# A two-layer encoder trunk on one core: the first four output tiles of four dense stages made row tile by row tile

## The chip, the core and the metric

The kernel runs on one core of a Trainium2 chip. The metric is the device time of one execution in microseconds, the median of the runs, lower is better. Weights, inputs and constants lie in device memory and are read in every execution.

## What is computed

Two layers over S = 256 tokens of width D = 2048. Layer 0 mixes tokens with a sparse attention, layer 1 with RWKV-7; behind each stands a squared-ReLU MLP of width 4·D. Every sub-layer is normalised, modulated by a conditioning vector and added to the residual:

```python
hmix = rms_norm(x) * (1 + sc1) + sh1
x = x + g1 * (dsa_mixer(hmix, ...) if i % 2 == 0 else rwkv7_mixer(hmix, ...))
hff = rms_norm(x) * (1 + sc2) + sh2
x = x + g2 * (jnp.square(jax.nn.relu(hff @ mlp_w1[i])) @ mlp_w2[i])
```

Of the RWKV mixer two projections matter here, `r = xr @ w_r` and `k = xk @ w_k`, with `xr = h + delta * mu[0]` and `xk = h + delta * mu[2]`, where `delta` is the token before minus the token. All products are taken with float32 accuracy.

## The kernel before, in words

**Tiles.** x and every activation lie transposed: 16 row tiles of 128 features by 256 tokens. A value is split into a high part that TensorE multiplies exactly and a low rest, so one term of a product is three matmuls: high weight by high activation (L184), high by low (L185), low by high (L186). Split tiles are called A, and o for the last four of a stage; plain ones B. `dense` (L188) makes one output tile of 128 features: it goes through all 16 row tiles of the input, 48 matmuls into one PSUM bank. So the first output tile can't be finished before the last input tile is there.

**Weights.** `Weights` (L84 to L97) brings a weight in pieces of 128 rows by 512 columns, 256 KB each: a DMA issued by SyncE, a cast to the high part on ScalarE (L92), a subtraction for the low part on VectorE or GpSimd (L94). In the MLPs, pieces 2 and 3 of every four are GpSimd's. High and low tiles live in a ring of 8 slots named w, in the MLPs with 2 more named x (tiles whi, wlo, xhi, xlo). For a stage of `dense` the host lays a weight out so that the 4 pieces of a load hold the 16 row tiles of one output tile.

**The MLP** (`mlp`, L341). The input tiles h are x times a scale, made on ScalarE (high, L355) and VectorE (low, L356) straight from the residual; the RMS factor is put in behind the matmul. `tally` (L287) sums the squares of x into ssq on GpSimd. `up` (L366) makes an output tile with `dense` and then, in the very first tile only, calls `rms` (L371): four small matmuls sum ssq over the partitions (L306), VectorE scales the sum (L266), GpSimd takes the power -1/2 (L268), and four matmuls spread it over the partitions (L283) into a bank that is copied to rb. Each output tile is then multiplied by rb (L375), rectified, squared and split. Banks go round as d, c, m (2 + 2 + 2 banks). `ada_due` puts a part of the modulation of a later stage in between: a load of 1 MB and a row product on VectorE (L224).

**The RWKV projections** (`rwkv_project`, L717). `rms` gives rb in PSUM; `normed` (L728 to L731) multiplies x by rb on VectorE (L730) and modulates; `delta` (L735) is GpSimd's; `mix` (L738) is a VectorE operation (L741) and a split (L197 on ScalarE, L198 on VectorE or GpSimd). After the 16 mixed tiles `xm` of r, a loop over 16 output tiles makes r (banks d and m), stores it, and adds the row tile's part of four low-rank products (L770 to L772, banks a, b, i, j). Then 16 mixed tiles for the keys, and a loop in which output tile f of the keys is made (bank d) and `elements` (L851) of tile f - 1 works on it: it copies the bank to SBUF (L890) and has a chain of VectorE, ScalarE and GpSimd operations behind it; its own matmuls are L863 to L867 and a product of the gate. Value tiles follow.

**The order.** The program text gives dependences and banks; a list scheduler sets each engine's order from it at build time. It already lets up to four output tiles run side by side where their inputs come slowly. Each engine then works its list in order.

Of the kernel before, what the change touches and what calls it, by code (L numbers as in the profile page):

```python
# [16 lines left out]
P = 128  # L17
D = 2048
S = 256
NS = S + 2  # L20
NF = D // P
# [18 lines left out]
AHEAD_UP = 2  # L40
# [61 lines left out]
class Trunk:  # L102
# [85 lines left out]
    def dense(s, w, movs, cols):  # L188
# [3 lines left out]
        return p  # L192

    def split(s, full, hi_from=None, eng=None, t=None):
        if t is None:
# [145 lines left out]
    def mlp(s, layer):  # L341
# [23 lines left out]

        def up(b, f):  # L366
            w = s.wload(s.io["mlp_w1"][layer, b * 16 + f])
            s.ada_due()
            p = s.dense(w, h, cols)
            if b == f == 0:  # L370
                nc.scalar.copy(rb, s.rms(D, [s.ssq, s.lsq]))  # L371
            u, r, q = s.B(), s.B(), s.B()
# [46 lines left out]


        for b in range(4):
            for f in range(AHEAD_UP if b else 0, 16):
                up(b, f)
            for f in range(AHEAD_UP if b < 3 else 0):
                up(b + 1, f)
            for g in range(4):
                down(b, g)
# [289 lines left out]
    def rwkv_project(s, keep):  # L717
# [6 lines left out]
        for t in hp:  # L724
            nc.vector.memset(t[:, 0:1], 0.0)
        rb = s.rms(D, [s.ssq, s.lsq])

# [28 lines left out]
        hid = [s.bank(k) for k in "ccij"]  # L756
        s.xv = []
        for f in range(NF):
            w = s.wload(io["b_w_r"][f])
            p = s.dense(w, xm, cols)  # L760
            t = s.B()
# [26 lines left out]
        s.pc = keep.tile([P, NF, 4], F32, name="pc")  # L788
        xm = [mix(i, 2, t=s.O() if i >= NF - NO else None) for i in range(NF)]
        for f in range(NF + 1):  # L790
            if f < NF:
                w = s.wload(io["b_w_k"][f])
                pk = s.dense(w, xm, cols)
            if f:
# [56 lines left out]
    def elements(s, f, pk, omka, wa0):  # L851
# [36 lines left out]

        k, kk, sq = s.B(), s.B(), s.B()
        nc.scalar.copy(k, pk)  # L890
        nc.vector.tensor_scalar(kk, k, s.v("k_k", f), None, op0=OP.mult)
# [309 lines left out]
def layout(inputs):  # L1201
# [4 lines left out]
    vec = lambda a: a.reshape(-1, P).T  # L1206

    def tiles(w, rows, cols):

# [3 lines left out]
    a = {}  # L1213
# [15 lines left out]
    a["c"] = ct(g["c"].reshape(-1))  # L1229
    a["mlp_w1"] = np.stack([tiles(w, 16, P) for w in g["mlp_w1"]])  # L1230

# [18 lines left out]
    for n in ("a_w_o", "b_w_o"):  # L1250
        w = g[n][0]
        a[n] = np.concatenate([tiles(w[b * 512:(b + 1) * 512], 4, 512) for b in range(4)])
    for n in ("b_w_r", "b_w_k", "b_w_v"):
        a[n] = tiles(g[n][0], 16, P)
    l1 = np.concatenate([g["b_w_w1"][0], g["b_w_a1"][0], g["b_w_g1"][0]], 1)
# [24 lines left out]
```

## Time and profile before

| | us |
|---|---|
| median of 3 runs | 2749.15 |
| lowest and highest | 2748.52, 2752.12 |
| the profiled execution | 2751.64 |
| its span (first to last instruction) | 2749.5 |
| TensorE busy | 2587.6 (94%) |
| VectorE busy | 1946.8 (71%) |
| GpSimd busy | 1344.8 (49%) |
| ScalarE busy | 1312.8 (48%) |

All times that follow come from the one profiled execution and count from the start of its span. Its own time is 2.49 us above the median. PE is TensorE's matmuls, DVE VectorE, ACT ScalarE, POOL GpSimd, SP SyncE. The granted clock is the share of full speed that TensorE's clock ran at: 1.00 is 2.4 GHz, 0.50 is 1.2 GHz. A matmul record lasts longer than the distance to the next, since matmuls are pipelined; what counts is the distance, about 0.12 us at full clock and 0.215 us at half, for 256 or 258 columns. A time in brackets behind a row is how long the engine had stood idle, with the instruction that ended it. The first MLP's matmuls begin at 459.36, those of r at 1245.95, those of the keys at about 1387; the second MLP's stage begins at about 1997.

### The profile page before, as it was taken

The page shows a single profiled execution, that of the slowest core. Times are in us where ns is not written, and L with a number is a line of the kernel's source. Part 1 is how long each engine was busy: PE and PEld are TensorE (multiplying, and loading weights), DVE is VectorE, ACT ScalarE, POOL GpSimd, SP SyncE. Part 2 cuts the span into 40 slices and gives each one's busy share as a digit, 9 for nine tenths or more (in the row PEclk, how much of TensorE's full clock was granted, in tenths as well). Part 3 has the DMA queues.
Part 4 walks back from the last instruction along what each step waited for, and adds up shares of the span by engine and source line. Part 5 has one row for each costly group of instructions (what it writes and reads, how often), then busy time and mean ns, then how long its engine had stood idle before and what let it go on. Part 6 is the DMA issues. An engine that isn't in the chain of part 4 may idle for free. (4 is left out here: it accounts for less than half of the span.)

```text
span 2749.5 us, 58296 instructions
## 1 busy us (share of the span) xinstructions
PE 2587.6 (94%) x21876; PEld 2282.0 (83%) x21876; DVE 1946.8 (71%) x3135; ACT 1312.8 (48%) x2836; POOL 1344.8 (49%) x1121
## 2 busy tenths in 40 slices
PE   6898999999999999998989899999899999999997
PEld 3566778988979979877978888888799898898996
DVE  2256568999999999968887666766688377473553
ACT  3334435445445444446655434444455555454553
POOL 1343227557567575665655412223565445444453
PEclk9999999999999999998999899999999999999998
DMA  9987745889899899864656623332466667555553
GB/s 366 411 338 260 259 152 178 297 302 371 282 312 363 282 343 328 290 205 128 194 171 228 206 83 95 103 118 92 148 233 222 224 220 238 192 182 192 187 185 103
DMA packets 263595, 624.33 MB, mean 227 GB/s; under 512 B 29328, under 2 KB 43024, under 8 KB 238352
## 3 DMA queue, kind: packets, MB, share of 16 engines
q1 hardware_dynamic: 256400, 608.03, 63.8%
q10 hardware_dynamic: 6912, 12.59, 1.3%
q8 instruction: 171, 2.80, 0.4%
q14 instruction: 112, 0.92, 0.1%
HBM read 603.72 MB, written 16.78 MB: 226 GB/s over the span
## 5 line engine op out<-in xcount | busy, mean ns | idle before, releaser
L94 POOL TENSOR_TENSOR wlo<-raw,whi 128x512 fp32r<-128x512 f32 x364 | 587.2, 1622 | 586.7 <-ACT whi L92 445.6
L92 ACT CAST whi<-raw 128x512 fp32r<-128x512 f32 x856 | 514.8, 618 | 410.4 <-PE ps_d L185 117.1
L94 DVE TENSOR_TENSOR wlo<-raw,whi 128x512 fp32r<-128x512 f32 x492 | 443.0, 908 | 206.4 <-ACT whi L92 200.2
L94 POOL TENSOR_TENSOR wlo<-more,whi 128x512 fp32r<-128x512 f32 x181 | 265.7, 1470 | 341.6 <-ACT whi L92 218.2
L224 DVE CUSTOM_DVE_ANT_0 araw<-araw,cb 128x2048 f32<-128x2048 f32 x124 | 335.7, 2720 | 5.6 <-DMA araw<-ada_w_in 5.5
L92 ACT CAST whi<-more 128x512 fp32r<-128x512 f32 x366 | 223.6, 618 | 201.8 <-PE ps_m L397 43.3
L94 DVE TENSOR_TENSOR wlo<-more,whi 128x512 fp32r<-128x512 f32 (+1 forms) x185 | 168.4, 912 | 116.6 <-ACT whi L92 112.8
L184 PE MATMUL ps_d<-A,whi 128*128 128x256 f32 x656 | 197.9, 303 | 7.8 <-ACT B L890 4.0
L185 PE MATMUL ps_d<-A,whi 128*128 128x256 f32 x656 | 191.6, 293 | 4.0 <-DVE A L198 3.7
L186 PE MATMUL ps_d<-A,wlo 128*128 128x256 f32 x656 | 190.5, 291 | 0.0
L376 ACT ACTIVATE B<-B,sm 128x256 f32<-128x256 f32 x128 | 65.1, 508 | 239.9 <-DVE B L375 239.6
L185 PE MATMUL ps_d<-h,whi 128*128 128x258 f32 x560 | 160.1, 286 | 2.1 <-DVE h L356 2.1
L184 PE MATMUL ps_d<-h,whi 128*128 128x258 f32 x560 | 159.3, 285 | 0.0
L186 PE MATMUL ps_d<-h,wlo 128*128 128x258 f32 x560 | 158.4, 283 | 0.3 <-DVE wlo L94 0.2
L186 PE MATMUL ps_m<-h,wlo 128*128 128x258 f32 x532 | 150.9, 284 | 3.7 <-DVE wlo L94 3.7
L184 PE MATMUL ps_m<-h,whi 128*128 128x258 f32 x532 | 152.0, 286 | 0.0
L185 PE MATMUL ps_m<-h,whi 128*128 128x258 f32 x532 | 151.6, 285 | 0.0
L184 PEld LDWEIGHTS ps_d<-A,whi 128*128 128x128 f32 x656 | 129.9, 199 | 23.3 <-issue 5.0
L377 DVE TENSOR_TENSOR B<-B 128x256 f32<-128x256 f32 x128 | 109.8, 857 | 55.2 <-ACT B L376 55.2
L185 PEld LDWEIGHTS ps_d<-A,whi 128*128 128x128 f32 x656 | 129.9, 198 | 7.5 <-DVE A L198 6.1
L186 PEld LDWEIGHTS ps_d<-A,wlo 128*128 128x128 f32 x656 | 129.7, 198 | 0.7 <-issue 0.5
L395 PE MATMUL ps_d<-whi,A 128*128 128x512 f32 x300 | 118.4, 395 | 3.9 <-DVE B L375 3.5
(541 smaller groups left out, 8204.2 us busy)
## 6 DMA issues: line engine op xcount, KB each, us to landing
araw<-ada_w_in SPq DMA_DIRECT2D x192, 1024.0 KB, 6.9
raw<-mlp_w_in SPq DMA_DIRECT2D x614, 256.0 KB, 4.2
more<-mlp_w_in SPq DMA_DIRECT2D x410, 256.0 KB, 4.2
raw<-b_w_r_in SPq DMA_DIRECT2D x64, 256.0 KB, 3.3
raw<-b_w_k_in SPq DMA_DIRECT2D x64, 256.0 KB, 3.4
raw<-b_w_v_in SPq DMA_DIRECT2D x64, 256.0 KB, 3.5
raw<-b_w_o_in SPq DMA_DIRECT2D x64, 256.0 KB, 3.4
hd<-A ACTq DMA_DIRECT2D x48, 256.0 KB, 4.1
```

Source lines behind the costliest of these rows:

```text
L92: t.nc.scalar.copy(hi[:, :n], r)
L94: e.tensor_tensor(lo[:, :n], r, hi[:, :n].bitcast(F32), op=OP.subtract)
L184: mm(out, wh, m[:, :w], start=i == 0, stop=False)
L185: mm(out, wh, m[:, w:], start=False, stop=False)
L186: mm(out, wl, m[:, :w], start=False, stop=i == n - 1)
L224: nc.vector.tensor_tensor_reduce(out=w, in0=w, in1=s.cb, scale=1.0, scalar=0.0, op0=OP.mult, op1=OP.add, accum_out=acc[:, k:k + 1])
L376: nc.scalar.activation(r, u, AF.Relu, bias=c)
L377: nc.vector.tensor_tensor(q, r, r, op=OP.mult)
L395: nc.tensor.matmul(p, hi, wh, start=n == 0, stop=False)
```

## The change

A new helper makes four output tiles at once: row tile by row tile of the input, in each the three matmuls of every one of the four output tiles, in four banks. A row tile of the input is then used 12 times in a row. It is called at four places: for tiles 0 to 3 of each MLP's first block (banks d, d, a, b), of r and of the keys (banks d, d, m, m). The host lays the weights of those four tiles out anew: a piece holds one row tile of 128 rows and the 512 columns of all four output tiles. Their bytes and the number of matmuls are the same as before.

Three things move with it. In the MLPs `rms` and the copy of rb stand behind the four tiles, and the four tiles' own processing behind that; `ada_due` stands ahead of the weight load. In the r stage rb is copied to SBUF, since its bank is wanted, so L730 reads two SBUF tensors where it read one of SBUF and one of PSUM. In the keys the four banks are copied to SBUF right after they are made, and `elements` of tiles 0 to 3 reads the copies.

```diff
+    def four(s, chunks, movs, banks):
+        mm = s.nc.tensor.matmul
+        n = movs[0].shape[-1] // 2
+        ps = [s.bank(k)[:, :n] for k in banks]
+        for i, ap in enumerate(chunks):
+            w = s.wload(ap)
+            for k in range(4):
+                first, last, m = not i + k, i * 4 + k == len(movs) - 1, movs[i * 4 + k]
+                for f, p in enumerate(ps):
+                    wh, wl = w.at(k * 512 + f * P)
+                    mm(p, wh, m[:, :n], start=first, stop=False)
+                    mm(p, wh, m[:, n:], start=False, stop=False)
+                    mm(p, wl, m[:, :n], start=False, stop=last)
+        return ps
...
-        def up(b, f):
-            w = s.wload(s.io["mlp_w1"][layer, b * 16 + f])
+        def up(b, f, p=None):
             s.ada_due()
-            p = s.dense(w, h, cols)
-            if b == f == 0:
-                nc.scalar.copy(rb, s.rms(D, [s.ssq, s.lsq]))
+            if p is None:
+                p = s.dense(s.wload(s.io["mlp_w1"][layer, b * 16 + f]), h, cols)
...
+        ps = s.four([s.io["mlp_w1"][layer, f] for f in range(4)], h, "ddcc")
+        nc.scalar.copy(rb, s.rms(D, [s.ssq, s.lsq]))
+        for f, p in enumerate(ps):
+            up(0, f, p)
         for b in range(4):
-            for f in range(AHEAD_UP if b else 0, 16):
+            for f in range(AHEAD_UP if b else 4, 16):
...
-        rb = s.rms(D, [s.ssq, s.lsq])
+        rb = s.B()
+        nc.scalar.copy(rb, s.rms(D, [s.ssq, s.lsq]))
...
+        ps = s.four([io["b_w_r"][f] for f in range(4)], xm, "ddmm")
         for f in range(NF):
-            w = s.wload(io["b_w_r"][f])
-            p = s.dense(w, xm, cols)
+            p = ps[f] if f < 4 else s.dense(s.wload(io["b_w_r"][f]), xm, cols)
...
+        ks = []
+        for p in s.four([io["b_w_k"][f] for f in range(4)], xm, "ddmm"):
+            ks.append(s.B())
+            nc.scalar.copy(ks[-1], p)
         for f in range(NF + 1):
-            if f < NF:
-                w = s.wload(io["b_w_k"][f])
-                pk = s.dense(w, xm, cols)
+            if f < 4:
+                pk = ks[f]
+            elif f < NF:
+                pk = s.dense(s.wload(io["b_w_k"][f]), xm, cols)
...
-        nc.scalar.copy(k, pk)
+        if f < 4:
+            k = pk
+        else:
+            k = s.B()
+            nc.scalar.copy(k, pk)
...
+    def four(w):
+        out = tiles(w, 16, P)
+        out[:4] = np.concatenate([tiles(w[q * 512:(q + 1) * 512, :512], 4, 512) for q in range(4)])
+        return out
```

What the scheduler makes of it is read from the order of the built kernels. A name's number tells its buffers apart; the changed kernel's lines are its own.

**TensorE, the start of the first MLP.** Before: the first output tile (ps_d) has one matmul pair from the high piece, then the second tile (ps_a) goes on alone through four input tiles h.

```order
L184 MATMUL ps_d_4943<-h_4786,xhi_4919 128x258
L185 MATMUL ps_d_4943<-h_4786,xhi_4919 128x258
L184 MATMUL ps_a_5044<-h_4786,whi_5016 128x258
L185 MATMUL ps_a_5044<-h_4786,whi_5016 128x258
L186 MATMUL ps_a_5044<-h_4786,wlo_5017 128x258
L184 MATMUL ps_a_5044<-h_4787,whi_5016 128x258
L185 MATMUL ps_a_5044<-h_4787,whi_5016 128x258
L186 MATMUL ps_a_5044<-h_4787,wlo_5017 128x258
L184 MATMUL ps_a_5044<-h_4788,whi_5016 128x258
```

In the changed kernel three of the four banks begin on the first input tile, and its low piece xlo is wanted at the seventh matmul:

```order
L205 MATMUL ps_d_4919<-h_4786,xhi_4923 128x258
L206 MATMUL ps_d_4919<-h_4786,xhi_4923 128x258
L205 MATMUL ps_a_4921<-h_4786,xhi_4923 128x258
L206 MATMUL ps_a_4921<-h_4786,xhi_4923 128x258
L205 MATMUL ps_d_4920<-h_4786,xhi_4923 128x258
L206 MATMUL ps_d_4920<-h_4786,xhi_4923 128x258
L207 MATMUL ps_d_4919<-h_4786,xlo_4924 128x258
L207 MATMUL ps_d_4920<-h_4786,xlo_4924 128x258
L207 MATMUL ps_a_4921<-h_4786,xlo_4924 128x258
L205 MATMUL ps_d_4919<-h_4787,whi_4929 128x258
```

Here the fourth bank, ps_b, comes later, when the mixer before has left it. So six matmuls stand ahead of the first one that needs xlo, where 12 stood before.

**TensorE, the RMS step of the first MLP.** Before: the end of the sums over ssq and lsq, and what follows them. In all, 42 matmuls of output tiles stand between the last sum (L306) and the spread (L283).

```order
L306 MATMUL ps_m_4992<-cst_82,ssq_87 128x1
L306 MATMUL ps_m_4992<-cst_82,lsq_88 128x1
L185 MATMUL ps_a_5044<-h_4801,whi_5034 128x258
L186 MATMUL ps_a_5044<-h_4801,wlo_5035 128x258
L186 MATMUL ps_d_5218<-h_4786,wlo_5192 128x258
L184 MATMUL ps_d_5218<-h_4787,whi_5191 128x258
```

In the changed kernel (L322 is L306 of before, L299 is L283) the sums stand behind the last matmul of the four tiles, and the spread follows at once:

```order
L322 MATMUL ps_m_5211<-cst_82,ssq_87 128x1
L322 MATMUL ps_m_5211<-cst_82,lsq_88 128x1
L299 MATMUL ps_m_5220<-cst_82,sm_5218 128x128 x2
L184 MATMUL ps_m_5478<-h_4786,whi_5454 128x258
L185 MATMUL ps_m_5478<-h_4786,whi_5454 128x258
L186 MATMUL ps_m_5478<-h_4786,wlo_5455 128x258
```

So the matmuls that stood between the sums and the spread are gone. The second MLP has the same two orders; there 28 matmuls stood between. On VectorE the row product L224 of before stands directly behind L266 in both kernels and in both MLPs. Ahead of the second MLP's stage, 34 matmuls of its own stand among the last of the mixer's output projection before, 48 in the changed kernel.

**ScalarE, the keys.** Before: the first key tile's copy (L890) stands behind the exponentials of its elements (L885, L886), and the second elements' activations follow.

```order
L885 ACT_TABLE_LOAD
L885 ACTIVATE A_16329<-B_16313 128x4x64
L886 ACTIVATE B_16330<-B_16313 128x256
L92 CAST whi_16527<-raw_16529 128x512
L890 COPY B_16335<-ps_d_16176 128x256
L92 CAST whi_16533<-raw_16535 128x512
L892 ACTIVATE B_16337<-B_16336 128x256
L871 ACTIVATE B_16458<-ps_m_16451,wa0_16037 128x256
```

In the changed kernel the four copies (L812) stand together, ahead of the first elements' activations (L895, which was L871):

```order
L92 CAST whi_16819<-raw_16821 128x512
L812 COPY B_16446<-ps_d_16154 128x256
L812 COPY B_16448<-ps_d_16155 128x256
L812 COPY B_16450<-ps_m_16156 128x256
L92 CAST whi_16825<-raw_16827 128x512
L812 COPY B_16452<-ps_m_16157 128x256
L92 CAST whi_16952<-raw_16954 128x512
```

So `elements` of tile 0 starts when all four key tiles are made, where it started with the first; TensorE's matmuls of the first elements (L863 to L867 before) stand behind the 192 matmuls of the four tiles too.

## Rows read from the trace of the kernel before

**Rows 1.** The page: the span and part 1, TensorE's row (busy, share, instructions)

```profile
span 2749.5 us, 58296 instructions
...
PE 2587.6 (94%) x21876; PEld 2282.0 (83%) x21876; DVE 1946.8 (71%) x3135; ACT 1312.8 (48%) x2836; POOL 1344.8 (49%) x1121
```

**Rows 2.** Busy time by stretch, PE: stretch, its length, busy (records), granted clock, DMA, GB/s

```profile
459.30:464.00 4.70, 2.30 (x12) 0.81 0.42 150
464.00:469.00 5.00, 4.96 (x23) 0.50 0.84 304
469.00:480.20 11.20, 9.11 (x63) 1.00 0.20 70
480.20:487.10 6.90, 6.85 (x58) 1.00 0.55 172
1250.50:1277.00 26.50, 24.65 (x187) 1.00 0.39 121
1277.00:1300.00 23.00, 18.90 (x129) 0.85 0.52 156
1386.70:1407.40 20.70, 17.75 (x120) 0.91 0.25 81
1397.20:1400.60 3.40, 3.38 (x16) 0.53 0.38 122
1995.20:2001.40 6.20, 5.62 (x24) 0.50 0.56 204
```

**Rows 3.** Timeline, PE: start, length, instruction, [idle before it <- what ended it]

```profile
462.99 0.55 PE L185 MATMUL ps_a<-h,whi 128*128 128x258 f32 x1 [2.31 <-DVE h L356]
...
1241.60 1.23 PE L283 MATMUL ps_m<-cst,sm 128*128 128x128 f32 x4 [1.04 <-POOL sm L268]
...
1277.50 0.39 PE L770 MATMUL ps_b<-A,lhi 128*128 128x256 f32 x1 [1.04 <-ACT A L197]
...
1292.62 0.58 PE L771 MATMUL ps_a<-A,lhi 128*128 128x256 f32 x1 [3.60 <-POOL A L198]
...
1395.89 0.39 PE L185 MATMUL ps_d<-A,whi 128*128 128x256 f32 x1 [1.53 <-DVE A L198]
...
1993.54 0.39 PE L184 MATMUL ps_d<-o,whi 128*128 128x256 f32 x1 [2.56 <-DVE x L436]
...
2021.20 0.71 PE L283 MATMUL ps_m<-cst,sm 128*128 128x128 f32 x4
```

**Rows 4.** Busy time by stretch, DVE, columns as in Rows 2

```profile
469.00:480.20 11.20, 11.20 (x12) 1.00 0.20 70
1250.50:1277.00 26.50, 25.05 (x46) 1.00 0.39 121
```

**Rows 5.** Timeline, DVE: the first low piece of MLP 0

```profile
463.16 0.82 DVE L94 TENSOR_TENSOR xlo<-more,xhi 128x512 fp32r<-128x512 f32 x1
```

**Rows 6.** Timeline, DVE: the second MLP's RMS step

```profile
2018.23 0.15 DVE L266 TENSOR_SCALAR sm<-ps_m 128x2 f32<-128x2 f32 x1
2018.30 2.28 DVE L224 CUSTOM_DVE_ANT_0 araw<-araw,cb 128x2048 f32<-128x2048 f32 x1
```

**Rows 7.** Timeline, POOL: the power in the r stage, a pair of splits, MLP 1's power

```profile
1240.84 0.71 POOL L268 TENSOR_TENSOR sm<-sm,cst 128x2 f32<-128x2 f32 x1 [2.19 <-DVE sm L266]
...
1287.63 4.93 POOL L198 TENSOR_TENSOR A<-B,A 128x256 fp32r<-128x256 f32 x1 [2.68 <-ACT A L197]
...
2018.46 2.69 POOL L268 TENSOR_TENSOR sm<-sm,cst 128x2 f32<-128x2 f32 x1 [0.70 <-DVE sm L266]
```

**Rows 8.** Costliest groups of 1245 to 1275, DVE: count, busy, mean ns, idle before

```profile
L741 DVE SCALAR_TENSOR_TENSOR B<-B,vec,h 128x256 f32<-128x256 f32 x19 | 13.0, 692 | 0.4 <-POOL B L735 0.4
...
L730 DVE TENSOR_TENSOR B<-x,ps_m 128x256 f32<-128x256 f32 x12 | 4.9, 407 | 0.0
```

**Rows 9.** Waits of PE, 1375 to 1420: total, times, longest

```profile
PE ps_d L185 <- DVE A L198: 2.5, 4, 1.5
```

**Rows 10.** One line, the key copies: durations min/median/max, first and last start

```profile
L890 ACT COPY B<-ps_d x16: 350/353/365, 1407.4 to 1542.2; 128x256 f32<-128x256 f32 x16
```

More of the change, by code (lines that the diff above doesn't have):

```diff
@@ L887, in elements @@
         nc.gpsimd.tensor_copy(s.pc[:, f, :].unsqueeze(2), pp[:, :, 64:65])
-        k, kk, sq = s.B(), s.B(), s.B()
-        nc.scalar.copy(k, pk)
+        kk, sq = s.B(), s.B()
+        if f < 4:
[3 more added lines that the diff above has]
+            nc.scalar.copy(k, pk)
         nc.vector.tensor_scalar(kk, k, s.v("k_k", f), None, op0=OP.mult)
@@ L1229, in layout @@
     a["c"] = ct(g["c"].reshape(-1))
-    a["mlp_w1"] = np.stack([tiles(w, 16, P) for w in g["mlp_w1"]])
+    a["mlp_w1"] = np.stack([four(w) for w in g["mlp_w1"]])
     a["mlp_w2"] = ct(g["mlp_w2"].reshape(2, 4, 4, 4, P, 4, 512).transpose(0, 1, 5, 2, 4, 3, 6)).reshape(2, 4, 4, 4, P, 2048)
@@ L1252, in layout @@
         a[n] = np.concatenate([tiles(w[b * 512:(b + 1) * 512], 4, 512) for b in range(4)])
-    for n in ("b_w_r", "b_w_k", "b_w_v"):
-        a[n] = tiles(g[n][0], 16, P)
+    for n in ("b_w_r", "b_w_k"):
+        a[n] = four(g[n][0])
+    a["b_w_v"] = tiles(g["b_w_v"][0], 16, P)
     l1 = np.concatenate([g["b_w_w1"][0], g["b_w_a1"][0], g["b_w_g1"][0]], 1)
```

## The prediction

> **What bounds the kernel now.** I read the page first: TensorE is busy for 2587.6 us of a span of 2749.5, 94% [rows 1]. The change leaves the number and the size of the matmuls alone, so it can only fill idle time of TensorE, run fewer matmuls at half clock, or do the reverse. Next I read TensorE's busy time stretch by stretch where a stage begins [rows 2], then the single waits there [rows 3], then the engine that feeds it [rows 4]. The reader should see two kinds of loss. In the first MLP, from 469.0 to 480.2, 63 matmul records stand where 11.2 us hold 94 at the full pace of 0.1195 us (6.9 us hold 58 in the next row); in the same stretch VectorE is busy for all 11.20 us [rows 2, 4]. It makes the input tiles, and TensorE waits for them. The second loss is the clock: after a wait of 2.31 us TensorE runs at 0.50, from 464 to 469, 23 records in 5 us [rows 2, 3]. Two other starts look the same: 2.56 us of waiting ahead of the second MLP, then 6.2 us at 0.50; 1.53 us in the keys, and the stretch around it at 0.91. A wait of 1.04 us at 1277.50 had no half clock behind it [rows 2, 3]. In 1250 to 1277 TensorE is 93% busy already, with VectorE busy for 25.05 of 26.5 us [rows 2, 4].
>
> **The change part by part.** All sums are differences against the profiled execution, 2751.64 us, which is 2.49 above the median of 2749.15. What a measurement can tell from no change is 0.2%, 5.5 us.
>
> *First MLP, more work for each input tile: -3.7.* With 12 matmuls for each input tile instead of what the scheduler found, TensorE needs 12 × 0.1195 = 1.43 us a tile; VectorE delivers the rest of the tiles by 480.2. So TensorE stops waiting: (94 - 63) × 0.1195 = 3.7 us [rows 2]. The bounds are 0, if VectorE's low weight pieces come late in its queue, and 3.7.
>
> *First MLP, the start: +0.7.* Only six matmuls stand ahead of the first low piece, which VectorE makes at 463.16 in 0.82 us, so until 463.98; 12 records ran there before, and a wait ended at 462.99 [rows 2, 3, 5]. Six matmuls at 0.1195 are the 0.7; the bounds are 0 and 2.7 (one half-clock stretch more, priced below).
>
> *Both MLPs, the RMS step: 2 × (+3.0).* Before, 42 and 28 output matmuls cover the chain of L266, L268 and L283: 6.9 us hold 6.85 busy [rows 2]. Now nothing stands between, so TensorE waits for the chain. Its price without cover is shown in the r stage: 1.04 us of waiting with a power of 0.71 us [rows 3, 7]. In the MLP that power lasts 2.69 us: VectorE begins a row product of 2.28 us 0.07 us after L266, and the order keeps it there [rows 6, 7]. So 1.04 + (2.69 - 0.71) = 3.0 us each. The bounds are 1.04 (the short power) and 3.5 (the second MLP's L266 came about half a microsecond late behind other work, 2018.23 [rows 6]). I take 3.0, since both orders leave the long power as it is.
>
> *Both MLPs, half clock behind that wait: 2 × (+2.7).* Waits of 2.31, 2.56 and 3.60 us all have a stretch of some 6 us at 0.50 behind them, one of 1.04 us has none [rows 2, 3]. 3.0 is on the side of the former. 24 records in 6.2 us at 0.50 would be 28 at a pitch of 0.215; 28 at 0.1195 are 3.35 us, so 6 us lose 2.7 [rows 2]. The bounds are 0 and 2.7 each.
>
> *Second MLP, more cover at its start: -1.7.* 48 of its matmuls stand among the mixer's last ones, 34 before; VectorE's residual chain (L436) sets the pace there, as the wait of 2.56 us shows [rows 3], so 14 more are done in idle time: 14 × 0.12. The bounds are 0 and the 2.56 itself.
>
> *r: 0.* The four tiles give TensorE little that it lacks, as it is 93% busy. But L730 changes its operand. With one in PSUM it took 407 ns each; L741 beside it, with its tensors in SBUF, averaged 692 ns [rows 8]. If L730 becomes such a row, 16 × 0.285 = 4.6 us are added to an engine without slack [rows 4], and the last mixed tile is that much later. TensorE has then done about 14 matmuls fewer at 1277 than before, 1.7 us. In the stretch behind, 1277 to 1300, it loses some 7 us to waits and half clock before, above all 3.60 us for a pair of GpSimd's splits, one of them 4.93 us long [rows 2, 3, 7]. Matmuls left over find room there, so I take the 1.7 back and write 0. The bounds are -7.5, when that stall with its half clock goes altogether, and +4.6, when it stays and the later tiles are paid in full.
>
> The Trainium skill, in "SBUF — State Buffer", section "SBUF: two separate sides", says why L741 would be slow beside GpSimd: the two share a port pair, a VectorE operation with two SBUF inputs takes it when GpSimd also reads SBUF, and the loser is blocked for the whole instruction. By that rule the copy of rb to SBUF is a cost that the diff doesn't show, and L730 would be the +4.6 just worked out; rows 8 agree with it so far, with 407 against 692.
>
> *Keys: -4.2.* The four waits for split tiles, 2.5 us, are covered by 12 matmuls per tile, and the half clock behind the longest of them (3.4 us at 0.50, of which half is lost, 1.7) goes with it [rows 2, 3, 9]. Against it stands that the elements of tile 0 begin with the last of four tiles, near 1414 by 192 matmuls, and not at 1407.4 [rows 10]. Since the fifth key tile and the value tiles behind give TensorE work, I price that at nothing. If that cover fails, up to 7 us come back. So the bounds are -4.2 and +3. The four copies, 0.35 us each [rows 10], are the same ones moved forward.
>
> *The rest: 0.* The stages behind are reordered by the scheduler but keep their work; in the MLPs' bulk TensorE is full, in the scan some 4 us either way are possible. That is a guess at its size; no row prices it.
>
> Sum: -3.7 + 0.7 + 6.0 + 5.4 - 1.7 + 0 - 4.2 = +2.5. Against the trace that is 2754.1; against the median, **2751.6 us**.
>
> **The rivals.**
>
> *Faster: the r stage's stall goes (2742).* With four tiles made early, later r tiles could cover the split pair at 1287.63. Then r gives -7.5, and 2751.6 - 7.5 = 2744.1; with one of the two half-clock stretches absent, 2.7 more, 2741.4. For it speaks that 18.90 of 23 us are busy there [rows 2]. Against it: the wait is for GpSimd's L198, a part of the low-rank work that the change leaves as it is, and which matmul stands behind it in order is the scheduler's choice.
>
> *Faster: the RMS step is cheap (2742).* If VectorE's row product is held up, so that the power takes 0.71 us as in the r stage [rows 7], each wait is 1.04 with no half clock behind it, and 2 × (3.0 - 1.04 + 2.7) = 9.3 us go: 2742.3. Against it: both long powers of before have that product beside them, and the order puts it there again [rows 6, 7].
>
> *Slower: L730 in SBUF sets the pace of r (2758 to 2763).* One mechanism: VectorE has under 6% idle in 1250 to 1277 [rows 4], so 16 slower operations push the last mixed tile by 4.6 us, and the low-rank work by as much. It decides if VectorE's L730 comes out above some 0.5 us: then r costs 4.6 and 2751.6 + 4.6 = 2756.2; where the keys' elements start late too (their 4.2 go and 3 come), 2763.4.
>
> *The change is hidden (2749).* The scheduler ran up to four tiles side by side anyway, so that filling and new waits are small on both sides: then all terms but the RMS steps vanish, and with short powers these are 2 × 1.04 = 2.1, covered by some of the 3.7. For it speaks 93% in r before the change; against it the 63 of 94 records and the plain order of the RMS step.
>
> **How the numbers follow.** Chances: my forecast, between 2746 and 2755, 0.38 (with the hidden case, 0.12 of it); the r stall gone 0.16 and the cheap RMS step 0.12, both under 2743.6, together 0.28; the slower, over 2754.6, 0.34. The first holds most of "same", which goes from 2743.6 to 2754.6. The range reaches from 2739 (the r stall gone, and half of the cheap RMS step's 9.3 with it: 2744.1 - 4.7 = 2739.4) to 2763 (the slower with late elements); I leave out a tenth on each side. So faster 0.28, same 0.38, slower 0.34.
>
> **What would show it.** Right, if the changed profile has 90 or more records in 469 to 480; a wait of TensorE at L299 near 490 and near 2027, each of about 3 us and for GpSimd's power, each with some 6 us at 0.50 behind it; L730's line (now in SBUF) at 0.5 to 0.7 us; and no wait for VectorE's splits at the keys' start. Wrong, if the spread's wait is 1 us or the clock behind it stays at 1.00, if L730 is still at 0.41, if 1277 to 1300 is full, or if the elements' waits grow where I priced them at nothing. If the MLPs' bulk or the scan moves by over 4 us, the sum fails there.

## The result and the profile after

The changed kernel is slower: median 2767.89 us (2764.04 to 2770.65, 4 runs) beside 2750.64 for the kernel before on the same chip; ratio 1.0059, 95% interval 1.0044 to 1.0074, so +16 us with 12 to 20. (A ratio times the median before gives the microseconds here and below.) Its profiled execution took 2767.95 us, 16.31 more than the one shown of before. The forecast was 2751.6, the range 2739 to 2763.

The page of the changed kernel, the span and TensorE's row (before: [rows 1]):

```profile
span 2766.2 us, 58247 instructions
...
PE 2593.9 (94%) x21876; PEld 2285.8 (83%) x21876; DVE 1946.8 (70%) x3135; ACT 1311.2 (47%) x2837; POOL 1341.9 (49%) x1121
```

The number of matmuls is the same, and TensorE is busy for 6.3 us more, at a mean granted clock of 0.962 where the trace of before has 0.967: matmuls at half clock last longer. The other 10 us are idle time.

TensorE's busy time by stretch in the changed kernel, columns as in [rows 2]. Its first MLP begins 1.4 us later than in the first trace with the same order ahead of it, so the stretches are shifted a little:

```profile
470.00:482.00 12.00, 12.00 (x99) 0.97 0.21 68
490.00:496.00 6.00, 1.45 (x13) 0.89 0.98 353
496.00:502.00 6.00, 6.00 (x31) 0.54 0.90 326
1280.00:1303.00 23.00, 20.22 (x153) 1.00 0.49 149
1391.00:1411.00 20.00, 20.00 (x149) 0.88 0.37 117
1411.00:1445.00 34.00, 30.05 (x245) 0.93 0.73 229
2043.00:2048.50 5.50, 2.09 (x17) 0.93 0.79 237
2048.50:2054.00 5.50, 5.50 (x38) 0.76 0.87 358
```

The first and the fifth row are what the change promises: 99 records in 12 us of the first MLP, where 63 stood in 11.2, and no idle time in the keys from 1391 on (149 records in 20 us, 120 in 20.7 before) [rows 2]. The second and third, seventh and eighth are the RMS step: an idle stretch, then half clock. The waits themselves, in TensorE's timeline of the changed kernel (L299 is the spread, L283 of before):

```profile
495.76 1.22 PE L299 MATMUL ps_m<-cst,sm 128*128 128x128 f32 x4 [4.55 <-POOL sm L284]
...
1602.10 0.70 PE L965 MATMUL ps_m<-B,cst 128*128 128x256 f32 x2 [1.29 <-DMA B<-hd]
...
2047.46 1.02 PE L299 MATMUL ps_m<-cst,sm 128*128 128x128 f32 x4 [3.41 <-POOL sm L284]
```

Three more waits bear on the forecast. In the first MLP's start TensorE waits for the third of the four banks, which the mixer's residual operation (L454, L436 of before) still reads; and in the keys two waits for split tiles stand just ahead of 1391, with the clock at 0.50 from 1386 to 1395.5:

```profile
464.68 0.58 PE L205 MATMUL ps_d<-h,xhi 128*128 128x258 f32 x1 [3.22 <-DVE x L454]
...
1388.36 0.80 PE L205 MATMUL ps_d<-A,whi 128*128 128x256 f32 x2 [1.58 <-ACT A L213]
1390.94 0.58 PE L206 MATMUL ps_d<-A,whi 128*128 128x256 f32 x1 [1.35 <-DVE A L214]
```

Where the whole went is read by comparing starts. For every kind of instruction (engine, line, operation) that occurs equally often in both kernels, the start of its k-th instance in one trace is set against that in the trace of before; the median over all that lie in 20 us is the lag there. The table has what the lag grew by in each stage. The first stage is the same code in the same order in all kernels, so its column is the spread of single executions. The other rows are the experiments below.

```
us against the   before   first   r      keys,     scan    start of  MLP 1,  whole
first trace      MLP 0    MLP            elements          MLP 1     rest
(time in it)     0-440    -1220   -1380  -1540     -1980   -2100     -2700
changed            1.4     1.9     1.3     1.7      9.6     3.0      -2.3    16.6
n1_ada            -5.6     2.2    -0.5     0.0     -4.0     0.4       1.4    -6.0
n2_omka            2.1    -2.0     0.8    -2.7      6.7    -0.4       0.2     4.5
e1_mlp            -2.9     0.7    -0.2     0.3      9.6     3.7      -2.3     8.8
e2_r              -3.3    -1.4     3.6    -1.8     13.6    -1.1      -2.3     7.3
e3_keys           -2.3    -1.7    -1.3     4.9      5.3    -0.7      -2.3     1.9
e4_mlp_rms_first  -1.2     8.8    -3.0     4.2     12.9    -2.7      -2.3    16.7
f1_mlp1            0.2    -2.1    -1.1     2.0     -2.3     2.8      -2.3    -2.9
f2_mlp1_cover      1.7    -1.9    -0.7    -0.1      2.2    -2.3      -2.3    -3.5
f3_rb             -2.9     1.0     3.9     2.0     33.0    -0.2       0.0    36.9
f4_keys2          -0.8     0.6     0.2     3.1      4.8    -0.4      -1.6     5.9
g1_after_omka      0.5     2.3     2.9     1.2     15.7     3.5      -2.3    23.8
g2_after_cover     1.8   -13.1     1.0     3.0      5.6    -1.4      -2.3    -5.3
```

So the largest part of the loss, 9.6 of 16.6 us, lies in the scan, whose code the change doesn't touch. Where the order is that of before, the same stage of two traces differs by up to 6 us (the scan: 411 to 417.5 us in four traces), so an entry of 2 us alone says little. Where two stages overlap, at 1380 and 1540, an entry also moves by 1 to 4 us with the place of the edge, and its neighbour moves the other way: e3's 4.9 and 5.3 are 3.0 and 7.1 if the edge is the first use of hd. The -2.3 in the last column belongs to an order: near 2300 TensorE waits 1.05 and 0.64 us for low weight pieces in the trace of before, and as long or longer, 1.1 and 0.6 to 1.9 us, in n1, n2 and f3, whose second MLP has the same order but for its first rows. Every kernel with tiles made at once has another order there and lacks these waits, also e2 and e3, which leave the second MLP's text alone.

What stands in the scan: the sync engine issues in order the loads of the value weights (L167) and of the elements' results hd, which `prepare` wants. Its timeline in the kernel before:

```profile
1578.54 5.12 SPq L167 DMA_DIRECT2D raw<-b_w_v_in  x2
1583.71 0.91 SPq L934 DMA_DIRECT2D A<-hd  x2
```

and in the changed kernel:

```profile
1585.87 9.35 SPq L167 DMA_DIRECT2D raw<-b_w_v_in  x3
1595.27 0.90 SPq L962 DMA_DIRECT2D A<-hd  x2
1596.27 0.38 SPq L167 DMA_DIRECT2D raw<-b_w_v_in  x1
1596.69 0.91 SPq L962 DMA_DIRECT2D B<-hd  x2
```

Three weight loads, each waiting for a free slot, now stand ahead of the hd load where two did; it is issued at 1596.69, and TensorE waits for it until 1602.10 and runs at half clock for a part of the time behind (0.83 in 1602 to 1612). That is one place; the lag grows by some 6 us around it, from 7.3 at 1560 to 13.5 at 1620, and by 2 more up to 1980. The same queue, three weight loads ahead of the hd load, stands in two of the experiments below that make no tile differently: TensorE waits there for 0.60 us in n2 and for 2.16 in f3, and in none of the four traces of the old order. TensorE's timeline in f3:

```profile
1599.92 0.48 PE L938 MATMUL ps_m<-B,cst 128*128 128x256 f32 x1 [2.16 <-DMA B<-hd]
```

### The profile page after: what moved, and what is told of

Same layout as the page of the kernel before. It is cut to its first block, busy times and chain, and to the rows that moved or that the text cites. A ratio compares the mean times of both kernels' runs of the same rounds, so it can differ in the third digit from the quotient of the medians.

```text
span 2766.2 us, 58247 instructions
## 1 busy us (share of the span) xinstructions
PE 2593.9 (94%) x21876; PEld 2285.8 (83%) x21876; DVE 1946.8 (70%) x3135; ACT 1311.2 (47%) x2837; POOL 1341.9 (49%) x1121
## 5 line engine op out<-in xcount | busy, mean ns | idle before, releaser
L94 POOL TENSOR_TENSOR wlo<-raw,whi 128x512 fp32r<-128x512 f32 x364 | 580.2, 1602 | 576.8 <-ACT whi L92 481.4
L94 DVE TENSOR_TENSOR wlo<-raw,whi 128x512 fp32r<-128x512 f32 x492 | 452.1, 927 | 213.5 <-ACT whi L92 208.3
L94 DVE TENSOR_TENSOR wlo<-more,whi 128x512 fp32r<-128x512 f32 (+1 forms) x185 | 157.3, 852 | 114.6 <-ACT whi L92 113.8
L184 PE MATMUL ps_d<-A,whi 128*128 128x256 f32 x584 | 175.6, 301 | 2.0 <-ACT B L918 1.2
L185 PE MATMUL ps_d<-A,whi 128*128 128x256 f32 x584 | 167.7, 287 | 0.0
L186 PE MATMUL ps_d<-A,wlo 128*128 128x256 f32 x584 | 167.6, 287 | 0.0
L186 PE MATMUL ps_d<-h,wlo 128*128 128x258 f32 x524 | 148.0, 282 | 4.6 <-DVE wlo L94 4.6
L184 PE MATMUL ps_d<-h,whi 128*128 128x258 f32 x524 | 148.7, 284 | 0.0
L185 PE MATMUL ps_d<-h,whi 128*128 128x258 f32 x524 | 148.7, 284 | 0.0
L184 PE MATMUL ps_m<-h,whi 128*128 128x258 f32 x512 | 147.3, 288 | 0.0
L185 PE MATMUL ps_m<-h,whi 128*128 128x258 f32 x512 | 146.8, 287 | 0.0
L184 PEld LDWEIGHTS ps_d<-A,whi 128*128 128x128 f32 x584 | 113.9, 195 | 17.3 <-issue 5.0
L410 PE MATMUL ps_m<-wlo,A 128*128 128x512 f32 x312 | 121.8, 390 | 1.5 <-DVE wlo L94 1.4
L411 PE MATMUL ps_m<-whi,A 128*128 128x512 f32 x312 | 121.5, 389 | 0.0
```

Source lines behind the costliest of these rows:

```text
L94: e.tensor_tensor(lo[:, :n], r, hi[:, :n].bitcast(F32), op=OP.subtract)
L184: mm(out, wh, m[:, :w], start=i == 0, stop=False)
L185: mm(out, wh, m[:, w:], start=False, stop=False)
L186: mm(out, wl, m[:, :w], start=False, stop=i == n - 1)
L410: nc.tensor.matmul(p, hi, wl, start=False, stop=False)
L411: nc.tensor.matmul(p, lo, wh, start=False, stop=n == 15)
```

## The experiments

**The parts alone.** Each of e1 to e3 keeps the change in one place and has the text of before in the others; the weights' layout goes with it.

```diff
 e1_mlp: r and the keys as before, rb of r in PSUM
 e2_r:   the MLPs and the keys as before
 e3_keys: the MLPs and r as before, rb of r in PSUM
```

> The four tiles at once in the two MLPs alone; r and the keys as before. Theory (each stage pays by itself, and the scan's shift comes from the keys): TensorE waits 3 to 5 us for the RMS chain at each of the two steps, about 6 us at half clock behind each; the start of the first MLP keeps 95 or more records in 469 to 482; no change between r's start and the second MLP; total +2 to +6 us. Rival (the loss in the scan is the scheduler's answer to any change ahead of it): the scan starts some 8 us late here too, total +10 to +14.

> The four tiles at once in r alone, with rb copied to SBUF; the MLPs and the keys as before. Theory: the multiplication by rb takes 0.5 to 0.6 us instead of 0.41, the last mixed tile of r comes 4 to 6 us later, the stage costs +2 to +4 us up to the keys, and the scan adds nothing: total +1 to +5. Rival (the scan's 8 us come from r or from any reordering): total +8 to +12.

> The four tiles at once in the keys alone, with the copies of the four banks. Theory: the first elements end some 15 us later, that lag is made up by tile 5, the elements end within 3 us of before, and the scan's beginning (1555 to 1640) then loses about 8 us, because the loads of the elements' results stand behind more value weights in the sync engine's queue: total +5 to +10. Rival (the scan's loss is not the keys'): total -4 to +2, as the predicted saving of 4 us at the start of the keys.

Measured: e1 1.0043 (1.0028 to 1.0058), +12 us; e2 1.0030 (1.0018 to 1.0041), +8; e3 1.0007 (0.9996 to 1.0019), +2. The rivals hold in e1 and e2; e3's total lies with its rival's, though its interval reaches the theory's 5. The RMS waits of e1 are there (5.07 and 3.41 us), and they cost 3.7 us in the second MLP and nothing that can be told in the first, but 9.6 us of e1 lie in the scan, behind an r and keys stage that are untouched. e2 has 13.6 there, e3 5.3, and 4.9 in the keys, where up to 3 were expected. Each part alone gives a scan about as long as the changed kernel's 424.1 us (424.8, 428.3 and 422.6, measured below), so the scan's loss isn't the keys' in particular, and the three parts add up to 22, not 16: a redrawn order doesn't add.

**The RMS step ahead of the four tiles.**

```diff
-        ps = s.four([s.io["mlp_w1"][layer, f] for f in range(4)], h, "ddcc")
         nc.scalar.copy(rb, s.rms(D, [s.ssq, s.lsq]))
+        ps = s.four([s.io["mlp_w1"][layer, f] for f in range(4)], h, "ddcc")
```

> As the kernel with the four tiles in the MLPs alone, but the RMS step stands ahead of the four tiles in the program text, so that its two short matmul groups lie among the 192 matmuls. Theory (the RMS wait and the half clock behind it eat what the four tiles gain): no wait over 1.5 us at the spread in either MLP, no half clock behind it, and 5 to 12 us faster than the version with the RMS step behind the tiles, so -6 to 0 against the kernel before. Rival (the wait is slack that the next stage gives back, since the weights set the pace behind): within 2 us of the version with the RMS step behind.

Measured: 1.0057 (1.0041 to 1.0073), no better than e1: a miss in the whole. By stage it is half right: the second MLP's start is 2.7 us shorter than before, 6.4 shorter than in e1. In the first MLP the power came late once more, since VectorE reached L282 only at 479.79, 5 us behind the last sum, after input tiles and weight pieces; the 31 matmuls between sums and spread didn't cover that, and the work behind lacked its weights. TensorE's waits there:

```profile
481.15 0.71 PE L299 MATMUL ps_m<-cst,sm 128*128 128x128 f32 x4 [2.80 <-POOL sm L284]
497.43 0.39 PE L186 MATMUL ps_m<-h,wlo 128*128 128x258 f32 x1 [2.51 <-DVE wlo L94]
```

**The kernel before once more, and with a neutral edit.** n1 has `ada_due` ahead of the weight load, as the change has it, which leaves the order of TensorE, VectorE and SyncE as it was, row for row. n2 moves two small operations:

```diff
 def rwkv_project(s, keep):
+        omka = s.tp.tile([P, 16], F32, name="omka")
+        nc.vector.tensor_scalar(omka, s.v("k_a", 0, 16), -1.0, 1.0, op0=OP.mult, op1=OP.add)
+        wa0 = s.tp.tile([P, 32], F32, name="wa0")
+        nc.vector.tensor_scalar(wa0, s.v("w0", 0, 32), 0.5, None, op0=OP.mult)
...
-        (the same four lines ahead of the keys)
```

> The kernel before with ada_due ahead of the weight load in the MLP's up, as the change has it, and nothing else of the change. The scheduler's order is the same, row for row, on TensorE, VectorE and SyncE. So it is a second look at the kernel before: time within 5 us of it, each stage's length within 2 us of the first trace, the scan (1540 to 1990) among them. If the scan here is 5 us or more longer than in the first trace, that trace was a lucky one and part of the scan's loss is not the change's.

> The kernel before with two small VectorE operations of the keys stage (omka and wa0, 16 and 32 columns) moved to the start of the RWKV projections. No work is added; the scheduler moves about 2,700 rows of TensorE's order behind that point. Theory (the scan's order in the kernel before is a good draw of the scheduler, and any reordering ahead of it costs some us there): the scan gets 4 to 12 us longer, total +4 to +12. Rival (the scan's loss comes from the four tiles themselves): within 2 us of the kernel before.

Measured: n1 ran once, 2745.60 us, 6 us under the first trace, its scan 4 us shorter; both are more than the 5 and 2 us that I had expected as spread, but the first trace was no lucky one. n2 1.0010 (0.9998 to 1.0021), between nothing and +6 us, so its whole decides between neither; its scan is 6.3 us longer than in the first trace, as the theory had it. The scan from the first use of hd to the last finished head, TensorE's busy time by stretch, first in the trace of before:

```profile
1564.16:1979.64 415.48, 404.64 (x7380) 0.96 0.31 100
```

n1, with the same order:

```profile
1560.39:1971.45 411.06, 400.09 (x7380) 0.98 0.32 101
```

n2, with the neutral edit:

```profile
1562.68:1984.46 421.78, 408.41 (x7380) 0.96 0.31 99
```

and the changed kernel:

```profile
1571.43:1995.54 424.11, 411.45 (x7381) 0.95 0.31 99
```

The work is the same in all four. The same measure in the other kernels: f1 413.0 and f2 417.5 (order of before up to the scan's end), f4 420.8, e3 422.6, e1 424.8, e4 428.2, e2 428.3. One pair is worth more than the rest: f4, which makes two key tiles at once, has the order of n2 in the scan, but for three rows of TensorE's and one of VectorE's that moved. Their scans take 420.8 and 421.8 us. So where the order is the same the lengths agree, with tiles made at once ahead of the scan or without.

**A barrier ahead of the scan,** in the kernel before (n3) and in the changed one (n4):

```diff
+            tc.strict_bb_all_engine_barrier()
             with t.phase("scan", a=23, b=13, m=0, g=(1, 2)):
```

> The kernel before with a barrier of all engines between the projections and the scan. It takes away the overlap of the two, and the scheduler starts the scan afresh. Both theories: 3 to 15 us slower than the kernel before. It is the base for the next kernel.

> The changed kernel with the same barrier. The scan's order is then the same as in the kernel before with the barrier for its first 887 matmul rows. Theory (the scan's loss is one of order alone): from the barrier to the second MLP the two take the same time within 2 us, and the whole differs by 5 to 9 us, what the MLPs, r and the keys cost. Rival (the four tiles leave something behind that the scan pays for): the scan is 6 us or more longer here too, and the whole differs by 12 to 18.

Measured: n3 1.0024 (1.0010 to 1.0039), n4 1.0064 (1.0051 to 1.0078) of the kernel before; n3 as expected, and between them 11 us, outside both expectations for n4 (5 to 9, 12 to 18). By the same measure the scan takes 436.8 us in n3 and 440.1 in n4, 3.3 apart, over the theory's 2 and under the rival's 6, where 6.6 to 13 lie between the changed kernel and the four traces of the old order. An order that begins alike takes away most of the difference but, at 11 us in the whole, not all that the change costs.

**The second MLP alone, without and with a bank for cover.** f1 has the four tiles in the second MLP only. f2 adds:

```diff
             nc.scalar.copy(rb, s.rms(D, [s.ssq, s.lsq]))
+            s.kinds = "i"
+            ps.append(s.dense(s.wload(s.io["mlp_w1"][layer, 4]), h, cols))
+            s.kinds = "dcm"
             for f, p in enumerate(ps):
                 up(0, f, p)
```

> The four tiles at once in the second MLP alone. The order up to the end of the scan is that of the kernel before, so the scan's draw does not enter. Theory (all six banks are held: four by the tiles, two by the RMS step; so no matmul can stand between its sums and its spread): TensorE waits 3.4 us at the spread, half clock behind it, and the whole is 3 to 6 us slower. Rival (the second MLP gives it back in its bulk, as the first does): within 1.5 us.

> As the one before, but the fifth tile goes to the bank ps_i, which the MLP leaves unused, so 31 of its matmuls stand between the sums and the spread. Theory (the missing bank is what costs in the second MLP): no wait over 1 us at the spread, no half clock behind it, and 3 to 6 us faster than the version without, so -2 to +1 against the kernel before. Rival (the cost lies elsewhere, in the start among the last output projections): still 2 us or more slower than before.

Measured: f1 1.0006 (0.9994 to 1.0017), so +2 us, between theory and rival, with 2.8 us lost at the MLP's start; f2 0.9981 (0.9972 to 0.9991), **5 us faster than the kernel before**, and 6 to 7 us below f1, somewhat more than the 3 to 6 expected. In f1 the spread waits, and half clock follows (TensorE's timeline, then its busy time):

```profile
2027.18 1.22 PE L299 MATMUL ps_m<-cst,sm 128*128 128x128 f32 x4 [3.41 <-POOL sm L284]
```

```profile
2020.00:2026.00 6.00, 3.77 (x33) 0.95 0.96 321
2026.00:2032.00 6.00, 4.82 (x22) 0.50 0.82 286
2032.00:2038.00 6.00, 6.00 (x51) 0.98 0.39 143
```

In f2 the same stretches are full:

```profile
2020.00:2026.00 6.00, 6.00 (x52) 1.00 0.83 265
2026.00:2032.00 6.00, 6.00 (x53) 1.00 0.84 285
2032.00:2038.00 6.00, 6.00 (x53) 1.00 0.75 250
```

So, with the RMS step behind the four tiles, the wait is one of banks. The four tiles hold d, d, a and b until rb is there, and the RMS step holds both m for its sums and its spread; a fifth tile has nowhere to go. ps_i lies unused in the MLP, and with it 31 matmuls stand in the gap. It isn't the only way: in e4, without that bank, 36 matmuls cover the second MLP's spread.

**rb in SBUF alone,** with no four tiles anywhere:

```diff
-        rb = s.rms(D, [s.ssq, s.lsq])
+        rb = s.B()
+        nc.scalar.copy(rb, s.rms(D, [s.ssq, s.lsq]))
```

> The kernel before with rb copied to SBUF in the r stage, and no four tiles anywhere. Theory: the multiplication by rb takes 0.5 to 0.6 us instead of 0.41, r's last mixed tile comes 2 to 4 us later and the stage is 1 to 3 us longer up to the keys (1380); the scan gets a new order by it and is 5 to 12 us longer than the 411 to 415 us of the kernel before. Rival (the copy costs nothing, the four tiles do): the stage up to 1380 within 0.5 us, the scan within 3 us.

Measured: 1.0084 (1.0065 to 1.0103), +23 us, more than the whole change. The r stage costs 3.9 us, more than the 1 to 3 expected and as much as all of e2's r; the scan is 33 us longer (448.4 us in this profile, which is the slowest of its 6 runs, 15 us above their median, so part of the 33 is that one run's). The line of the multiplication in f3, minimum, median and maximum:

```profile
L731 DVE TENSOR_TENSOR B<-x,B x16: 411/418/830, 1241.4 to 1261.9; 128x256 f32<-128x256 f32 x16
```

Eleven of the 16 take what they took from PSUM, five twice that; the mean is 544 ns where before has 409, so 2.2 us in all. The copy itself puts off the first of them by 0.4 us. Which ones are slow can be read from the traces. VectorE and GpSimd in the changed kernel, at two of its L749 (L730 of before):

```profile
1248.14 0.79 POOL L754 TENSOR_TENSOR B<-h 128x256 f32<-128x256 f32 x1
1248.38 0.83 DVE L749 TENSOR_TENSOR B<-x,B 128x256 f32<-128x256 f32 x1
...
1249.89 0.41 DVE L749 TENSOR_TENSOR B<-x,B 128x256 f32<-128x256 f32 x1
```

and at one of the kernel before, whose second operand lies in PSUM:

```profile
1248.94 0.80 POOL L735 TENSOR_TENSOR B<-h 128x256 f32<-128x256 f32 x1
1249.19 0.41 DVE L730 TENSOR_TENSOR B<-x,ps_m 128x256 f32<-128x256 f32 x1
```

All five slow ones of f3 and all four of the changed kernel begin while an operation of GpSimd is under way, and none of the fast ones does. In the kernel before 8 of 16 begin so, and none of these takes over 0.41 us. So the theory's place was right, and r pays for the operand, not, as far as a spread of some 2 us lets one tell, for the four tiles; the size in the scan was not foreseen.

**Two tiles at once in the keys instead of four.**

```diff
-            for k in range(4):
+            for k in range(8):
...
-                    wh, wl = w.at(k * 512 + f * P)
+                    wh, wl = w.at(k * 256 + f * P)
...
-        for p in s.four([io["b_w_k"][f] for f in range(4)], xm, "ddmm"):
+        for p in s.four([io["b_w_k"][f] for f in range(2)], xm, "dd"):
```

> Two tiles of the keys at once instead of four (pieces of two row tiles by 256 columns), MLPs and r as before. Theory (the keys lose because the first elements start only when all tiles made at once are there): the first key copy comes within 4 us of the kernel before, the elements end (1555 in the first trace) 2 us or more earlier than with four at once. Rival (the loss is the order of the elements, not their start): the elements end as with four at once, some 4 us late.

Measured: 1.0022 (1.0011 to 1.0033). The first copy comes at 1406.8 (1407.4 in the first trace), yet the elements lose 3.1 us, against 4.9 in e3: 1.8 us, under the 2 that the theory asked for (2.6 and 3.0 at the first use of hd). TensorE's longest waits in f4, 1400 to 1560:

```profile
PE ps_d L184 <- ACT B L915: 9.4, 5, 2.7
PE ps_m L884 <- ACT B L892: 2.4, 2, 1.6
```

It waits for key banks to be copied out (L915 is L890 of before), 9.4 us where before has 4.0 and e3 7.7. So a late start of the elements isn't needed for the loss; what makes these copies late stays open. In the changed kernel the same waits come to 1.2 us, and e4, whose keys are those of before, loses 4.2 us in the same column; so these copies aren't shown to be the cause, and the key tiles made at once aren't either.

**The changed kernel with the neutral edit, and with the free bank in both MLPs.** g1 is the changed kernel with n2's edit, g2 the changed kernel with f2's.

> The changed kernel with the same two small VectorE operations moved as in n2 (omka and wa0, to the start of the projections). No work changes; the scheduler draws a new order of the scan for the changed kernel. Theory (the largest part of the change's loss is the scan's order, which any edit ahead redraws): the scan's length differs by 3 us or more from the 424 us of the changed kernel, and the whole moves with it, while the second MLP's start still costs 3 to 5 us. Rival (the loss belongs to the four tiles): the scan stays within 3 us of 424.

> The changed kernel with the fifth tile of both MLPs in the unused bank ps_i, so that matmuls stand between the sums and the spread. Theory: no wait over 1 us at either spread, the second MLP's start 4 to 6 us shorter than in the changed kernel; the first MLP's gives its gain back in its bulk, where the weights' DMA sets the pace; apart from a new draw of the scan the whole is 3 to 7 us faster than the changed kernel, so still 8 to 14 us slower than the one before. Rival (the first MLP's wait is paid in full too): 9 to 13 us faster than the changed kernel.

Measured: g1 1.0059 (1.0041 to 1.0077), the same as the changed kernel in the whole, while its scan differs by 6.8 us in its trace; the expected move of the whole did not show, and the second MLP's start costs 3.5 us, as expected. g2 0.9972 (0.9959 to 0.9985), **8 us faster than the kernel before** and the fastest here, 24 faster than the changed kernel, well past both expectations. The second MLP's spread no longer waits and its start is 4.4 us shorter, as expected; the first MLP's spread still waits 2.34 us, where under 1 was expected. The scan in its trace, 1.4 us from the changed kernel's:

```profile
1555.32:1978.04 422.72, 407.11 (x7380) 0.97 0.32 99
```

Its largest gain lies in the first MLP, -13.1 us against +1.9. I had taken that stage to be paced by its weights; it isn't quite. TensorE's longest waits between 500 and 1225 in the changed kernel:

```profile
PE ps_d L410 <- DVE wlo L94: 7.2, 3, 5.3
PE ps_d L409 <- DVE B L389: 6.7, 1, 6.7
PE ps_d L186 <- DVE wlo L94: 4.6, 3, 1.7
PE ps_a L426 <- DVE y L418: 3.4, 2, 2.1
```

and in g2:

```profile
PE ps_d L409 <- DVE B L389: 5.9, 1, 5.9
PE ps_d L410 <- POOL wlo L94: 4.6, 3, 2.6
PE ps_a L186 <- DVE wlo L94: 2.8, 2, 1.5
PE ps_d L410 <- DVE wlo L94: 2.0, 4, 1.1
```

The waits of the low weight pieces have become shorter, and some have moved to other pieces. Between 640 and 1225, well behind the edit, TensorE is idle for 11.8 us where the changed kernel has 17.9, at a mean granted clock of 1.00 against 0.99. The likely reason is that the fifth tile at the start redrew the order of the whole MLP, to the good this time; no run here shows that apart from the bank itself.

## Why the prediction was wrong

*First MLP, more work for each input tile: right.* 99 records in 12 us; the h waits are gone behind 464.68. By the matmuls done (each weighted with its columns) TensorE lags by 1.6 us at 450 and leads by 2.6 at 490, 4.2 gained where -3.7 and +0.7 forecast 3.0.

*The start, +0.7: about right in size, with another cause.* The wait is 3.22 us where it was 2.31. But only four matmuls stand ahead of it, and it isn't for xlo: the third bank is free only when L454 has read it, at 464.63.

*The RMS step, 2 × 3.0: right in kind, undersized in the first MLP.* Measured 4.55 and 3.41 us. From the lead of 2.6 at 490 TensorE goes to a lag of 5.6 at 500, so wait and half clock cost 8.2 us in the first MLP, 5.7 forecast. The power lasts 2.69 us beside the row product, as forecast from [rows 6, 7]. What I left out is what stands ahead of L266 on VectorE in the first MLP; its timeline in the changed kernel:

```profile
490.93 1.95 DVE L94 TENSOR_TENSOR wlo<-raw,whi 128x512 fp32r<-128x512 f32 x2 [2.13 <-ACT whi L92]
492.80 0.15 DVE L282 TENSOR_SCALAR sm<-ps_m 128x2 f32<-128x2 f32 x1
492.86 2.27 DVE L240 CUSTOM_DVE_ANT_0 araw<-araw,cb 128x2048 f32<-128x2048 f32 x1
```

The sums are there at 491.2, and L282 stands behind two weight pieces until 492.80. *Half clock behind the waits, 2 × 2.7: right in the first MLP and in f1, too much in the second MLP of the changed kernel;* 31 and 38 records in 6.0 and 5.5 us, where full pace gives 50 and 46, are 2.3 and 1.0 us, and f1 has 0.50 for the whole of 2026 to 2032. I also had the reason incomplete, by naming the order alone: where the step stands behind the four tiles, the banks leave the order no choice (f2).

*Where the loss is paid.* In the second MLP it is paid: +2.8 to +3.7 in f1, e1 and the changed kernel, +4.0 forecast. In the first MLP the loss net of the gain, 4 us at 500 (5.6 less 1.6), has fallen to 1.9 at its end, so about half is given back, where I had its 2.7 paid in full. That 2.7 and 1.9 lie close is luck: gain and loss were both larger than forecast.

*r, 0: wrong by 1 to 4 us.* The stretch 1277 to 1300 did become fuller (20.22 of 23 us at full clock, before 18.90 at 0.85), but the price of rb in SBUF is 3.9 us by f3, close to the upper bound of 4.6. The mean of L730's successor is 518 ns in the changed kernel and 544 in f3, so the operation itself adds 1.7 and 2.2 us, where the bound had 4.6: only the instances that meet GpSimd are slow, not all 16. The Trainium skill's rule ("SBUF — State Buffer", section "SBUF: two separate sides") is borne out: the four instances that begin during a GpSimd operation take 828 to 832 ns, the other twelve 410 to 425.

*Keys, -4.2: wrong.* From 1391 on the start is as forecast, with 149 records in 20 us; but two waits for split tiles, 2.9 us in all, and half clock stand ahead, and I had them gone. By the matmuls done the lag still falls by some 4 us between 1380 and 1420, and it is more than back by 1450. So what lies behind gives the gain back: 4.9 us lost in e3 over the keys and the elements, 1.7 in the changed kernel. I had priced the elements at nothing, because TensorE has other work. In e3 it waits in order for the key banks' copies (7.7 us, 4.0 before), in the changed kernel hardly (1.2); which wait costs it there is open.

*The rest, 0 with 4 us either way: the step that failed.* The scan takes 424.1 us instead of 411 to 417.5, and 9.6 of the 16.6 us are lost there. I had noted that the scheduler reorders it, called my figure a guess, and not made it a rival. Ten kernels without a barrier have another order of the scan than the one before (nine orders, as n2 and f4 share one), and all ten take 420.8 us or more; in n2 and f3 no tile was made differently. That such a loss comes without the four tiles is shown by f3 and, less sharply, n2, and that equal orders take equal time by n2 and f4; that the four tiles have no share of their own in the changed kernel is not shown (n3 and n4 leave 3.3 us open), nor is which of the order's many differences costs what, beyond the hd loads above. The other end of this step, the MLPs' bulk, was "full" in the forecast: there a new order gave 2.3 us back near 2300.

Of the rivals, the slower one (r paced by rb in SBUF, keys late, 2756 to 2763) was nearest in sign and had its mechanism confirmed by f3, but not the size. (Its heading says 2758; its own sum begins at 2756.2.)

## What to carry to other kernels

Where a list scheduler orders everything, an edit in one stage is also a new draw for all stages behind it; take that draw as a term with its own spread, measured by a neutral edit, before crediting a local gain of a few microseconds. Count the banks at a step whose result everything waits for: one free bank turned a small loss into a gain of 5 us in f2; g2's gain is larger, but most of it lies in a first MLP that runs differently as a whole. And where tiles are made at once, look at who consumes them and in what order their banks come free.

## What the runs showed of the hardware

The power of 128 by 2 values takes 0.71 us alone and 2.69 beside the row product [rows 7]. GpSimd's timeline in the changed kernel:

```profile
493.02 2.69 POOL L284 TENSOR_TENSOR sm<-sm,cst 128x2 f32<-128x2 f32 x1 [1.30 <-DVE sm L282]
```

The row product of VectorE runs from 492.86 to 495.13, and the power ends 0.58 us behind it: it reads as if it began to work only when the product was done, which no run here shows directly. The other way round, a VectorE multiplication with both inputs in SBUF took 0.83 us instead of 0.41 wherever it began during a GpSimd operation, and 0.41 with one input in PSUM (f3 above). The clock of one order is not fixed either. TensorE's busy time at the same place of the scan, first in the trace of before:

```profile
1636.00:1646.00 10.00, 10.00 (x58) 0.50 0.01 2
```

and in n1, whose order is the same, row for row:

```profile
1632.00:1642.00 10.00, 10.00 (x163) 1.00 0.26 80
```

TensorE is busy throughout in both, and 0.9 us of idle time, 0.6 at most in one piece, stand in the 10 us before in both (9.14 and 9.12 us busy); yet one runs at half clock and the other does not, and 5.9 us of lag come of it. The changed kernel has 20 us at 0.54 near there (1640 to 1660). So a scan's length in one trace carries some 6 us of chance, which is why the lengths of two orders are compared here over several traces and kernels, and why the medians of many runs, not a trace, say what a kernel costs.
